# New operation figures in a list-scheduling planner, with the scaled x blocks and last-value copies on ScalarE

## The chip, the cores and the metric

The kernel runs on one core of one Trainium2 chip. A time is device microseconds (us) of one execution, the median of the runs shown. Engines: TensorE (PE in the profile; its weight loads are PEld), VectorE (DVE), ScalarE (ACT), GpSimd (POOL) and SyncE (SP), whose queue issues the transfers.

## The reference

One layer of a streaming encoder, for 1024 prompt positions and 32 sample positions over 512 cached ones, with shared weights. D_MODEL is 1024, eight heads of 64 in each of two mixers, a feed-forward width of 4096, all in fp32.

```
z = rmsnorm(x) @ w_in            # q,k,v of mixer A; indexer queries, key, head weights; q,k,v of mixer B; two gates
score = sum_h relu(q_i[h] @ k_i) * w_i[h];  idx = top_k(score)        # mixer A: which keys a query sees
o_a = softmax(q_a @ k_a[idx] / 8) @ v_a[idx]                          # with QK-norm and rotary
o_b = a @ v_b,  a = exp(log_sigmoid(s) - tail of softplus(s))         # mixer B: stick-breaking, s = q_b @ k_b / 8
h = x + W_out(sigmoid(g_A) * (o_a @ W_bA) + sigmoid(g_B) * (o_b @ W_bB))
y = h + W_down(relu(W_up rmsnorm(h))^2)
```

## The kernel before

All 1056 positions are one list of columns: eight tiles of 128 prompt positions and a ninth of 32 sample positions. Matmuls run on numbers split in two: a value is rounded to a shorter format (the high half, names ending in h) and the rest is kept as a second tile (the low half, names ending in l). A product is three matmuls, wh·xh, wh·xl and wl·xh. So each operand costs a rounding (ScalarE, or rarely VectorE or GpSimd) and a subtraction (VectorE or GpSimd) before TensorE can use it.

The stages: the index stage (first 70 us or so) normalises x block by block and projects it on the index queries and keys, in two parts; then mixer B's projections, index scores and a bitwise top-k search, mixer A's projections and gates; the attention of both mixers, in which gate products and the first part of the feed-forward network are woven in as filler; the rest of the feed-forward in a scheme with fewer products (quarter sums of the weights), to the end.

**What sets the order.** The kernel doesn't issue instructions as it is written. Every operation is recorded in a Plan (lines 109 to 425), which keeps data dependences between recorded operations and issues them by a list scheduler: `run` takes the engine that is free first, and from its ready operations the one with the best rank (FAST, PREP, MAIN, FILL, SLOW) and, within a rank, the first recorded. `cost` (line 223) gives each operation two numbers, how long it keeps its engine and how long until its result is there, by engine, operation and n, the elements in a partition; `after` adds SLACK, 300 ns, to each hand-over between engines. [...] The figures therefore decide nothing on the chip but the order on each engine; all operations are issued at line 416, which is why the profile has that line almost everywhere, and one goes by tiles.

**What the change touches.** `normalise` (line 717) loads eight blocks k of x for a group of tiles, in five groups of 128, 256, 128, 256 and 288 columns. Of each it makes xh, x scaled by g_mix and rounded, and xl = x*g_mix - xh on VectorE. For the first group and for k below 6 xh is made on ScalarE, for k = 6 and 7 of the other four groups on GpSimd, as a TENSOR_SCALAR. `index_weights` (805) loads the eight blocks of the index weights, rounds each (ih) and subtracts (il): il on GpSimd for odd k, on VectorE for even k. `index_projection` (821) multiplies them into bank s, after which VectorE makes the products ta and tb with the rotary tables, GpSimd adds them (rr, ka), TensorE transposes rr (bank t), and ScalarE and VectorE make both halves of qi. `unit` makes both halves of a 512-column weight block (wst to wh on ScalarE, wl on GpSimd). `spread_rs` (775) brings the reciprocal norms into rows: rsb is transposed into t, ScalarE copies it to rb, and VectorE multiplies the projections in bank pj by rb (zb). `project_v` (1030) copies the last column of each tile of v (vl, 128x8) from vt on VectorE.

## Time and profile before

| | |
|---|---|
| median of the runs shown | 1709.43 us (1708.81 to 1710.45) |
| the profiled execution | 1708.92 us, span 1707.1 us |
| mean granted TensorE clock | 1.000 |
| busy: PE, DVE, ACT, POOL | 1693.5, 1199.8, 1054.7, 887.8 us |
| transfers | 302.41 MB, mean 177 GB/s |

A row of instructions reads: line, engine, operation, out<-in by the program's names, shapes, count | busy us, mean ns of one | idle time of the engine just before, and what ended it. A row of the timeline begins with its start and its duration in us, and has the idle time before it in brackets. In the table of windows an engine's busy us stand beside the length of the window. Matmuls overlap, the end of one with the start of the next, so TensorE's starts tell more than its idle time.

### The profile page before, as it was taken

The numbers are of one execution on the slowest core, as the hardware profiler recorded it, in microseconds if no ns is written. First come the engines' busy times: TensorE is split into PE (matmuls) and PEld (weight loads), VectorE is DVE, ScalarE is ACT, GpSimd is POOL, SyncE is SP. The second block draws the span as 40 slices with busy tenths as digits, with TensorE's granted clock in tenths as the row PEclk, the third lists the DMA queues.
The fourth block names the chain that finished last, engine by engine and source line by source line (L and its number), as shares of the span: only waits on it lengthen the run. The fifth ranks groups of instructions, "written<-read, shape, count | busy, mean of one in ns | idle before, by whom it ended". The sixth has DMA issues, their size and how long they took to land.

```text
span 1707.1 us, 33451 instructions
## 1 busy us (share of the span) xinstructions
PE 1693.5 (99%) x11442; PEld 1574.0 (92%) x11442; DVE 1199.8 (70%) x2606; ACT 1054.7 (62%) x2319; POOL 887.8 (52%) x791
## 2 busy tenths in 40 slices
PE   8999999999999999999999999999999999999999
PEld 7989999999999988998888888889899999999998
DVE  8467788999656655987485776686765784767577
ACT  6656799873255777665465565575745675747473
POOL 5442343435433465235654443567667894646563
PEclk9999999999999999999999999999999999999999
DMA  7453453354577677544667465586576665555665
GB/s 225 122 149 102 140 160 99 114 164 147 163 197 196 166 207 236 156 146 132 195 210 231 144 206 179 187 276 210 193 249 181 193 183 175 173 173 173 173 188 172
DMA packets 195962, 302.41 MB, mean 177 GB/s; under 512 B 36048, under 2 KB 67376, under 8 KB 195792
## 3 DMA queue, kind: packets, MB, share of 16 engines
q1 hardware_dynamic: 195504, 299.94, 58.1%
q8 instruction: 90, 1.47, 0.4%
q14 instruction: 80, 0.66, 0.1%
q10 hardware_dynamic: 288, 0.34, 0.1%
HBM read 212.39 MB, written 87.70 MB: 176 GB/s over the span
## 4 chain that ended last, share of the span: by engine, by line
PE 92%; DVE 3%; POOL 1%; issue 1%; DMA 1%; ACT 1%; ACTq 0%; POOLq 0%; SPq 0%; DVEq 0%
PE pj L416 66%; PE s L416 14%; PE t L416 5%; PE o L416 4%; PE pd L416 2%; DVE p L416 1%; DVE xl L416 1%; POOL wl L416 1%; DVE tt L416 0%; DMA k<-cka 0%; DMA x<-xT 0%; DVE pj L416 0%; DVE wl L416 0%; POOL xh L416 0%; DVE more L416 0%
## 5 line engine op out<-in xcount | busy, mean ns | idle before, releaser
L416 PE MATMUL pj<-xh,wh 128*128 128x272 f32 (+2 forms) x1795 | 599.6, 335 | 1.2 <-DVE zb L416 0.8
L416 PE MATMUL pj<-xl,wh 128*128 128x272 f32 (+2 forms) x1795 | 599.2, 335 | 0.5 <-DVE xl L416 0.5
L416 PE MATMUL pj<-xh,wl 128*128 128x272 f32 (+2 forms) x1795 | 598.7, 334 | 0.0
L416 POOL TENSOR_TENSOR wl<-wst,wh 128x512 fp32r<-128x512 f32 x233 | 316.2, 1362 | 315.7 <-ACT wh L416 264.0
L416 PEld LDWEIGHTS pj<-xh,wh 128*128 128x128 f32 x1795 | 337.3, 188 | 30.5 <-DVE y L416 1.2
L416 PEld LDWEIGHTS pj<-xl,wh 128*128 128x128 f32 x1795 | 337.8, 188 | 29.3 <-DVE xl L416 0.7
L416 PEld LDWEIGHTS pj<-xh,wl 128*128 128x128 f32 x1795 | 337.4, 188 | 28.9
L416 ACT CAST wh<-wst 128x512 fp32r<-128x512 f32 x253 | 155.8, 620 | 113.2 <-PE pj L416 71.5
L416 POOL TENSOR_TENSOR wl<-raw,wh 128x512 fp32r<-128x512 f32 x98 | 132.2, 1354 | 87.8 <-ACT wh L416 61.4
L416 ACT CAST wh<-raw 128x512 fp32r<-128x512 f32 x148 | 91.4, 623 | 84.4 <-PE pj L416 54.6
L416 DVE TENSOR_TENSOR tt<-t,tt 128x512 fp32r<-128x512 f32 (+2 forms) x168 | 101.3, 621 | 45.3 <-ACT tt L416 44.3
L416 ACT CAST tt<-t 128x512 fp32r<-128x512 f32 (+2 forms) x168 | 86.5, 537 | 65.7 <-PE t L416 38.8
L416 ACT ACTIVATE junk<-score,cand 128x384 bf16<-128x384 f32 (+1 forms) x124 | 116.0, 935 | 3.2 <-DVE cand L416 1.0
L416 DVE TENSOR_TENSOR_SCAN p<-p 128x896 f32<-128x896 f32 (+6 forms) x66 | 101.2, 1562 | 9.8 <-ACT p L416 9.6
L416 PE MATMUL pj<-gl,wh 128*128 128x272 f32 x352 | 101.2, 288 | 0.0
L416 PE MATMUL pj<-gh,wh 128*128 128x272 f32 x352 | 101.2, 288 | 0.0
L416 PE MATMUL pj<-gh,wl 128*128 128x272 f32 x352 | 101.0, 289 | 0.0
L416 PEld LDWEIGHTS o<-tt,v 128*128 128x128 f32 x640 | 90.8, 188 | 8.3 <-DVE o L416 0.9
L416 PE MATMUL o<-tt,v 128*128 128x256 f32 (+1 forms) x640 | 97.7, 277 | 0.4 <-DVE tt L416 0.3
L416 PE MATMUL s<-k,q 128*128 128x384 f32 (+5 forms) x384 | 92.8, 353 | 0.3 <-issue 0.2
L416 POOL TENSOR_TENSOR wl<-rb,wh 128x512 fp32r<-128x512 f32 x49 | 68.4, 1397 | 42.0 <-ACT wh L416 41.9
L416 PE MATMUL s<-wh,xh 128*128 128x256 f32 x320 | 90.1, 285 | 0.0
(415 smaller groups left out, 4021.2 us busy)
## 6 DMA issues: line engine op xcount, KB each, us to landing
q<-dq SPq DMA_DIRECT2D x64, 256.0 KB, 5.2
raw<-w_up SPq DMA_DIRECT2D x52, 256.0 KB, 3.1
raw<-w_down SPq DMA_DIRECT2D x52, 256.0 KB, 3.0
k<-dk SPq DMA_DIRECT2D x48, 256.0 KB, 4.3
v<-dv SPq DMA_DIRECT2D x48, 256.0 KB, 3.5
wst<-w_g SPq DMA_DIRECT2D x42, 256.0 KB, 3.5
wst<-w_up SPq DMA_DIRECT2D x37, 256.0 KB, 2.9
wst<-w_down SPq DMA_DIRECT2D x36, 256.0 KB, 3.6
```

The source lines that it names most:

```text
L416: fn(*args, **kw)
```

## The change

Three things. First, figures in `cost`: VectorE's tensor_scalar has a fixed part of 200 ns for 160, its tensor_tensor_reduce 150 for 230; ScalarE's fixed part is 160 for 195 where the input lies in PSUM, and it is counted as free 110 ns (95 from SBUF) ahead of its result for 90; GpSimd's two-input operations are 200 + 2.14 n for 330 + 1.9 n, its tensor_scalar 270 + 0.85 n for 300 + 0.9 n. Second, all xh of `normalise` are made on ScalarE, eight more than before. Third, the four odd il go from GpSimd to VectorE, and the four copies vl from VectorE to ScalarE.

```
-            d = 300 + 0.9 * n if op in ("tensor_scalar", "memset") else 330 + 1.9 * n
-            return d - 30, d
+            d = 270 + 0.85 * n if op == "tensor_scalar" else 70 + 0.95 * n if op == "memset" else 200 + 2.14 * n
+            if op == "tensor_scalar" and out.dtype == F32R:
+                d = 230 + 3.2 * n
+            return d - 35, d
...
-                if sl[0] == 0 or k < 6:
+                if True:
                     nc.scalar.activation(xh, x32[:, kk, :n], AF.Copy, scale=self.gm[:, k:k + 1])
                 else:
                     nc.gpsimd.tensor_scalar(xh, x32[:, kk, :n], self.gm[:, k:k + 1], None, op0=ALU.mult)
...
-            (nc.gpsimd if k % 2 else nc.vector).tensor_sub(l, st, h.bitcast(F32))
+            nc.vector.tensor_sub(l, st, h.bitcast(F32))
...
-            nc.vector.tensor_copy(self.vl[:, p], vt[:, 127:SEQ:128])
+            nc.scalar.copy(self.vl[:, p], vt[:, 127:SEQ:128])
```

The number of matmuls and of transfers stays the same; their order does not. Three places follow, with the program's names and their buffer numbers (il1 is the low half of index weight block 1, xl0 the low half of x for the first 512 columns, x32 a loaded block pair, s a bank of the index projection). Lines are L416 before and L419 now.

VectorE in the first tile of the index stage, before:

```order
L416 TENSOR_TENSOR il0_245<-ist_243,ih0_244 128x328
L416 SCALAR_TENSOR_TENSOR xl0_222<-x32_242,gm_68,xh0_221 128x128 x2
L416 SCALAR_TENSOR_TENSOR xl0_222<-x32_249,gm_68,xh0_221 128x128
L416 TENSOR_TENSOR il2_252<-ist_250,ih2_251 128x328
L416 SCALAR_TENSOR_TENSOR xl0_222<-x32_249,gm_68,xh0_221 128x128
L416 SCALAR_TENSOR_TENSOR xl0_222<-x32_256,gm_68,xh0_221 128x128
L416 TENSOR_TENSOR il4_259<-ist_257,ih4_258 128x328
L416 SCALAR_TENSOR_TENSOR xl0_222<-x32_256,gm_68,xh0_221 128x128
L416 SCALAR_TENSOR_TENSOR xl0_222<-x32_263,gm_68,xh0_221 128x128
L416 TENSOR_TENSOR il6_266<-ist_264,ih6_265 128x328
```

VectorE there now:

```order
L419 TENSOR_TENSOR il1_248<-ist_246,ih1_247 128x328
L419 SCALAR_TENSOR_TENSOR xl0_222<-x32_242,gm_68,xh0_221 128x128 x2
L419 SCALAR_TENSOR_TENSOR xl0_222<-x32_249,gm_68,xh0_221 128x128
L419 TENSOR_TENSOR il2_252<-ist_250,ih2_251 128x328
L419 SCALAR_TENSOR_TENSOR xl0_222<-x32_249,gm_68,xh0_221 128x128
L419 TENSOR_TENSOR il3_255<-ist_253,ih3_254 128x328
L419 SCALAR_TENSOR_TENSOR xl0_222<-x32_256,gm_68,xh0_221 128x128 x2
L419 TENSOR_TENSOR il4_259<-ist_257,ih4_258 128x328
L419 TENSOR_TENSOR il5_262<-ist_260,ih5_261 128x328
L419 SCALAR_TENSOR_TENSOR xl0_222<-x32_263,gm_68,xh0_221 128x128 x2
L419 TENSOR_TENSOR il6_266<-ist_264,ih6_265 128x328
L419 TENSOR_TENSOR il7_269<-ist_267,ih7_268 128x328
```

The four odd il stand between the xl, and the last of them, il7, is the last of the tile's VectorE work; on TensorE its matmul now follows that of ih7 directly, where three matmuls of the next two tiles stood between.

GpSimd from its first il on, before:

```order
L416 TENSOR_TENSOR il7_269<-ist_267,ih7_268 128x328
L416 TENSOR_SCALAR xh0_221<-x32_278,gm_68 128x256 x2
L416 TENSOR_TENSOR rr_273<-ta_271,tb_272 128x256
L416 TENSOR_TENSOR ka_241<-ta_271,tb_272 128x64
L416 TENSOR_SCALAR xh0_221<-x32_292,gm_68 128x128
L416 TENSOR_TENSOR wl_343<-wst_341,wh_342 128x512
L416 TENSOR_TENSOR rr_282<-ta_280,tb_281 128x256
L416 TENSOR_TENSOR ka_241<-ta_280,tb_281 128x64
```

GpSimd there now:

```order
L419 TENSOR_TENSOR rr_273<-ta_271,tb_272 128x256
L419 TENSOR_TENSOR ka_241<-ta_271,tb_272 128x64
L419 TENSOR_TENSOR wl_343<-wst_341,wh_342 128x512
L419 TENSOR_TENSOR rr_282<-ta_280,tb_281 128x256
L419 TENSOR_TENSOR ka_241<-ta_280,tb_281 128x64
```

Both il and xh are gone, and what stood behind them follows at once; the eight xh stand on ScalarE behind those of blocks 4 and 5 of their group.

ScalarE where the reciprocal norms are spread (rb), with the casts of the next weights (wh), before:

```order
L416 COPY rb_225<-t_1161 128x32
L416 CAST qi_235<-t_407 64x2x32 x2
L416 CAST wh_1200<-wst_1199 128x512
L416 CAST wh_1215<-wst_1214 128x512
L416 COPY rb_225<-t_1160 128x512
L416 CAST zz_1177<-zb_1176 128x272
```

ScalarE there now:

```order
L419 COPY rb_225<-t_1162 128x32
L419 CAST qi_235<-t_407 64x2x32 x2
L419 CAST wh_1201<-wst_1200 128x512
L419 COPY rb_225<-t_1161 128x512
L419 CAST wh_1216<-wst_1215 128x512
L419 CAST zz_1178<-zb_1177 128x272
```

The second large copy to rb has moved ahead of a weight cast.

## The prediction

> **What bounds the kernel now.** I read the page first, then a table of windows by stage, then TensorE's waits, and last the timelines at the places where those waits fall. The page's busy line, and the chain that ended last:

> ```profile
> PE 1693.5 (99%) x11442; PEld 1574.0 (92%) x11442; DVE 1199.8 (70%) x2606; ACT 1054.7 (62%) x2319; POOL 887.8 (52%) x791
> PE 92%; DVE 3%; POOL 1%; issue 1%; DMA 1%; ACT 1%; ACTq 0%; POOLq 0%; SPq 0%; DVEq 0%
> ```

> TensorE is the bound: 1693.5 of 1707.1 us, at a granted clock of 1.00. The change issues the same matmuls in another order, so it can move the time only by the 13.6 us in which TensorE is idle, and by the little that such a pause hides. Where those lie, by stage (length, then each engine's busy us; the last window runs 0.9 us past the end of the span):

> ```profile
> 0.00:8.50 8.50, 3.22 (x11) 2.92 (x12) 4.40 (x14) 5.25 (x14) 2.15 (x6) 1.00 0.77 220
> 8.50:40.00 31.50, 29.50 (x183) 26.70 (x182) 29.74 (x60) 21.93 (x59) 23.28 (x27) 1.00 0.74 229
> 40.00:100.00 60.00, 59.16 (x428) 55.50 (x428) 31.49 (x93) 35.48 (x89) 23.94 (x31) 1.00 0.49 138
> 100.00:520.00 420.00, 420.00 (x2884) 390.97 (x2884) 326.66 (x860) 271.06 (x658) 167.62 (x162) 1.00 0.48 142
> 520.00:800.00 280.00, 279.27 (x1853) 254.72 (x1853) 206.27 (x383) 187.32 (x417) 125.55 (x119) 1.00 0.64 181
> 800.00:1400.00 600.00, 599.99 (x3702) 542.14 (x3701) 399.02 (x769) 355.32 (x697) 374.71 (x305) 1.00 0.63 201
> 1400.00:1708.00 308.00, 302.34 (x2393) 301.08 (x2391) 202.24 (x432) 178.35 (x390) 170.58 (x144) 1.00 0.59 176
> ```

> The columns are PE, PEld, DVE, ACT, POOL. The first 8.5 us lose 5.28 us to the first loads, which the change does not touch. The index stage to 40 us idles 2.00 us, and VectorE is busy there for 29.74 of 31.50 us: it is what TensorE waits for. From 40 to 100 us 0.84 us are idle, from 100 to 520 nothing, from 520 to 800 0.73 us, from 800 to 1400 0.01, and the rest is the last output and one pause. The longest of TensorE's waits say the same (total us, times, longest):

> ```profile
> PE s L416 <- ACT xh L416: 5.6, 2, 5.3
> PE s L416 <- DVE xl L416: 1.3, 2, 0.7
> PE pj L416 <- DVE zb L416: 0.8, 1, 0.8
> PE pj L416 <- DVE xl L416: 0.5, 1, 0.5
> PE o L416 <- DVE tt L416: 0.3, 1, 0.3
> ```

> The two waits for xl, the low half of x, are worth more than their idle time. On TensorE's timeline, at three places of the index stage:

> ```profile
> 16.57 0.31 PE L416 MATMUL s<-il,xh 128*128 128x328 f32 x1
> 17.00 0.42 PE L416 MATMUL s<-ih,xl 128*128 128x328 f32 x1
> ...
> 24.11 0.31 PE L416 MATMUL s<-ih,xl 128*128 128x328 f32 x1
> 25.06 0.42 PE L416 MATMUL s<-ih,xl 128*128 128x328 f32 x1 [0.64 <-DVE xl L416]
> 25.31 0.31 PE L416 MATMUL s<-ih,xh 128*128 128x328 f32 x1
> ...
> 31.40 0.31 PE L416 MATMUL s<-il,xh 128*128 128x328 f32 x1
> 32.36 0.57 PE L416 MATMUL s<-ih,xl 128*128 128x328 f32 x2 [0.65 <-DVE xl L416]
> ```

> The reader should look at starts, not at idle time. A matmul follows the one before by 0.15 us when nothing waits (25.31, then 25.46). From 24.11 to 25.06 are 0.95 us, so 0.80 are lost where 0.64 show as idle, and the next start comes 0.10 late as well: 0.90 in all, 0.26 more than is shown. By the same count 32.36 loses 0.91 and 17.00, which shows no idle time, 0.28 + 0.10 = 0.38.

> **Part by part. The x blocks.** Why is xl late? GpSimd and VectorE at those places:

> ```profile
> 21.47 0.69 POOL L416 TENSOR_SCALAR xh<-x,gm 128x128 fp32r<-128x128 f32 x1
> 22.13 2.59 POOL L416 TENSOR_TENSOR wl<-wst,wh 128x512 fp32r<-128x512 f32 x2
> ...
> 17.07 0.34 DVE L416 SCALAR_TENSOR_TENSOR xl<-x,gm,xh 128x128 fp32r<-128x128 f32 x1
> ...
> 22.20 1.38 DVE L416 SCALAR_TENSOR_TENSOR xl<-x,gm,xh 128x128 fp32r<-128x128 f32 x1
> ...
> 30.63 1.39 POOL L416 TENSOR_TENSOR wl<-wst,wh 128x512 fp32r<-128x512 f32 x1
> ...
> 30.41 1.89 DVE L416 SCALAR_TENSOR_TENSOR xl<-x,gm,xh 128x256 fp32r<-128x256 f32 x2
> ```

> The xl of block 7 needs GpSimd's xh, which ends at 22.16; by then GpSimd is in wl, and xl takes 1.38 us where the same form takes 0.34 undisturbed. That is 1.04 us, and the next xl, for which TensorE waits at 25.06, comes that much later. At 30.63 the two xl of blocks 6 and 7 meet another wl, which had queued behind two xh, and end at 32.30: that is the wait at 32.36. With the eight xh on ScalarE both causes go: xh is ready earlier, and GpSimd does its wl ahead of these xl. I take both waits and the 0.38 at 17.00 (an xl behind GpSimd's xh too) as gone: -0.90 - 0.91 - 0.38 = -2.19. VectorE stays nearly full here, so other rr, ka and wl can still hold some xl: the bounds are 0 and -2.19, and I keep -2.0 because the 1.04 us given back at 22.20 are more than either wait.

> What it costs on ScalarE: eight instructions, at most 0.532 us each by the row below, 4.3 us. ScalarE is busy for 21.93 of the stage's 31.50 us, so 9.6 us are free and I put it at nothing. Without that cover (ScalarE's own queue: qi, wi and the wh of w_ib stand behind them) up to 4.3 us would be late; w_ib is first used after 44 us.

> ```profile
> L416 ACT ACTIVATE xh<-x,gm 128x288 fp32r<-128x288 f32 x6 | 3.0, 532 | 1.3 <-DMA x<-xT 1.3
> L416 POOL TENSOR_TENSOR il<-ist,ih 128x328 fp32r<-128x328 f32 x4 | 3.8, 946 | 6.7 <-ACT ih L416 6.7
> L416 DVE TENSOR_TENSOR il<-ist,ih 128x328 fp32r<-128x328 f32 x4 | 2.0, 490 | 0.0
> ...
> 10.03 0.89 POOL L416 TENSOR_TENSOR il<-ist,ih 128x328 fp32r<-128x328 f32 x1 [0.47 <-ACT ih L416]
> ...
> 10.04 1.03 DVE L416 SCALAR_TENSOR_TENSOR xl<-x,gm,xh 128x128 fp32r<-128x128 f32 x1
> ```

> **The il.** Four low halves of the index weights leave GpSimd (3.8 us) and add 4 x 0.490 = 1.96 us to VectorE, in the first tile, where nothing covers VectorE. Against that, an xl beside GpSimd's il took 1.03 instead of 0.34: 0.69 back, and four il stand in that tile, so at most 4 x 0.69 = 2.8. VectorE comes out between -0.8 and +1.96. But the last il is now behind all of VectorE's work of the tile, and the row order has TensorE use it directly after ih7, where three matmuls of the next tiles stood between: I take +0.3, with ends -0.8 and +1.96.

> [...]

> ```profile
> 13.79 0.47 DVE L416 SCALAR_TENSOR_TENSOR xl<-x,gm,xh 128x256 fp32r<-128x256 f32 x1
> ...
> 13.85 2.11 POOL L416 TENSOR_SCALAR xh<-x,gm 128x256 fp32r<-128x256 f32 x2 [2.93 <-DMA x<-xT]
> ```

> This xl has two SBUF inputs, ran beside xh and took 0.47 all the same. So I count no hold-up beside xh as given back; if xl were held there, all of the stage's waits would go, which is the first rival.

> **The copies of the last values.** Four VectorE copies leave:

> ```profile
> L416 DVE COPY vl<-vt x4: 172/801/951, 120.7 to 253.1; 128x8 f32<-128x8 f32 x4
> ```

> At most 3.8 us of VectorE, all between 120 and 254 us, where TensorE is never idle (420.00 of 420.00). Zero, cover or no cover; on ScalarE they come between casts for TensorE, and a wait of 0.3 us each (the o wait above) would be the upper end, 1.2.

> **The new figures.** They reorder without adding work, most of all in the attention from some 470 to 965 us. One place where TensorE waits and the order changes in a clear way is the end of the first q projection:

> ```profile
> 84.06 0.60 PE L416 MATMUL t<-ident,rsb 128*128 128x128 f32 x4
> 86.06 0.50 PE L416 MATMUL pj<-xh,wh 128*128 128x512 f32 x1 [0.83 <-DVE zb L416]
> ...
> 84.31 0.62 ACT L416 CAST wh<-wst 128x512 fp32r<-128x512 f32 x1 [0.93 <-PE pj L416]
> 84.95 0.58 ACT L416 COPY rb<-t 128x512 f32<-128x512 f32 x1
> ```

> The transposes end at 84.66; rb starts at 84.95 because a cast of a weight is ahead of it. In the new order rb comes first: -0.3 (ends 0 and -0.93, the wait with its late second start). What is late next is zb, after rb. For the attention I take zero: its waits in 520 to 800 us are 0.73 idle, a new order removes some and makes others, so -1.3 to +1.3 (0.73 and two hidden 0.26).

> Sum: -2.0 + 0.3 + 0 - 0.3 + 0 = -2.0; the profiled execution took 1708.92 us (span 1707.1, 1.8 around it), which makes 1706.9. The median of the runs shown is 0.51 above that execution, so I predict 1707.4, 0.12% below 1709.43. About 0.2%, 3.4 us, is what a measurement of this kernel can tell from no change, so my forecast is: within it, on the fast side.

> **Rivals.** *All of the stage's waits go* (faster by over 0.2%): VectorE is freed by more than I count, every xl beside an xh included, and the 2.00 idle plus 0.26 for each of four shown waits (3.0) go, with 0.93 at 86 us: 1709.43 - 3.9 = 1705.5. [...] For it: VectorE is busy for 94% of that stage. Against it: rr, ka and wl stay on GpSimd and go on holding xl.

> *Nothing is gained*: the first tile costs the full 1.96 and the xl are held elsewhere by the same wl, which only move: 1709.43 - 2.0 + 1.96, some 1709.4. For it: GpSimd's wl are as many as before. Against it: the 1.03 beside il.

> *The attention runs out of margin* (slower): GpSimd's TENSOR_TENSOR is now counted by 200 + 2.14 n, 902 ns for 128x328, while that row's mean is 946. A low half that comes late is met by TensorE in order, and each such wait costs 0.3 (the o wait above) + 0.26 = 0.56. It decides only where the lateness passes the 300 ns of slack that the plan adds to each hand-over. To come out 0.2% slower it takes (3.4 + 2.0) / 0.56, ten such waits; with eleven it is 1707.4 + 6.2 = 1713.6. For it: TensorE's order changes most there. Against it: before, TensorE idled 0.73 us in 280 with the same slack.

> **How the numbers follow.** My forecast 0.42, all waits gone 0.30, nothing gained 0.18, attention 0.10. Faster by over 0.2% takes the first rival and a little of mine: 0.32; slower is the attention alone, nearly: 0.09; the rest, 0.59, is within. The range reaches from the first rival less 1.3 for the attention, 1704.2, and 0.6 below that for the il's better end, 1703.6, to nothing gained plus 1.3, 1710.7; it leaves out the attention's case and the far end of the first rival.

> **What would show it.** Right: in the changed profile PE's idle time in 8.5 to 40 us near 0.8 instead of 2.00, no wait for xl over 0.3 us after 20 us, VectorE's xl mean near 0.4 for 128x128, the wait for zb at 86 us shorter by 0.3, nothing idle from 100 to 520 us, and 0.7 +- 0.5 from 520 to 800. Wrong: a wait for il or xl of over 1 us in the first 13 us (the il), ScalarE's xh as TensorE's releaser after 15 us (the cover), or several idle us from 520 to 965 (the attention).

## The result, and the profile after

The changed kernel takes 1718.92 us (median of 6 runs, 1716.23 to 1723.23) against 1709.67 us for the kernel before (6 runs, 1708.81 to 1710.45). The ratio is 1.0059, 95% interval 1.0049 to 1.0069: slower by 9 us, where I had said 1707.4 and a range up to 1710.7. The profiled execution took 1717.92 us, its span 1716.1.

The busy line of the page after, then the table of windows of the changed kernel by the same stages (PE, PEld, DVE, ACT, POOL, the granted clock, the DMA share, GB/s; the last window is 9 us longer):

```profile
PE 1696.2 (99%) x11442; PEld 1577.4 (92%) x11442; DVE 1195.0 (70%) x2606; ACT 1057.8 (62%) x2331; POOL 883.7 (51%) x779
```

```profile
8.50:40.00 31.50, 29.13 (x177) 26.43 (x177) 28.46 (x59) 23.73 (x65) 14.07 (x17) 1.00 0.73 229
40.00:100.00 60.00, 59.67 (x432) 55.96 (x431) 31.55 (x94) 36.24 (x91) 22.58 (x30) 1.00 0.47 136
100.00:520.00 420.00, 417.17 (x2854) 387.54 (x2852) 330.01 (x856) 269.91 (x660) 165.18 (x162) 1.00 0.49 142
520.00:800.00 280.00, 277.12 (x1851) 254.88 (x1850) 198.38 (x379) 184.18 (x412) 132.31 (x117) 0.99 0.63 176
800.00:1400.00 600.00, 599.61 (x3672) 540.34 (x3671) 393.64 (x762) 353.76 (x690) 370.52 (x303) 1.00 0.63 201
1400.00:1717.00 317.00, 310.29 (x2457) 309.04 (x2455) 208.36 (x443) 184.71 (x405) 178.84 (x150) 1.00 0.59 175
```

TensorE's idle time went from 2.00 to 2.37 us in the index stage, from 0.84 to 0.33 up to 100 us, from 0 to 2.83 up to 520 us, from 0.73 to 2.88 up to 800 us and from 0.01 to 0.39 up to 1400 us. The clock column shows something new: 0.99 in one stage. TensorE's waits in the changed kernel:

```profile
PE s L419 <- ACT xh L419: 6.3, 2, 5.3
PE pj L419 <- POOL wl L419: 1.9, 2, 1.5
PE o L419 <- POOL vcs L419: 1.8, 1, 1.8
PE t L419 <- DVE az L419: 1.4, 1, 1.4
PE s L419 <- DVE xl L419: 1.1, 3, 0.7
PE t L419 <- POOL qk L419: 0.7, 1, 0.7
PE o L419 <- DVE o L419: 0.7, 1, 0.7
```

Few and single pauses, then, at places where the kernel before has none. Counting lost starts as in the prediction (the time from one matmul's start to the next, over the normal step), the matmul of the same number starts 0.7 us later than before at 45 us, 0.2 at 97, 3.5 at 446, 8.0 at 1394, and the last one 9.0 us later. Five losses of 0.8 us or more after 100 us (at 371, 397, 550, 712 and 1411 us) make 7.0 of it, and a stretch at half clock behind the one at 550 makes 1.55 more (last section). The longest losses are 1.61 us at 371 us, 2.02 at 550 and 1.69 at 1411; each has its own story, and the three timelines of the changed kernel show them. At 371, 550 and 1411 us, on TensorE and the engines beside it:

```profile
367.29 1.78 DVE L419 TENSOR_SCALAR pen<-score,tfa 128x1024 f32<-128x1024 f32 x1
368.48 0.58 ACT L419 CAST az<-t 128x512 fp32r<-128x512 f32 x1
369.10 1.66 DVE L419 CUSTOM_DVE_ANT_0 pen<-pen,score 128x1024 f32<-128x1024 f32 x1
369.63 2.25 POOL L419 TENSOR_TENSOR wl<-wst,wh 128x512 fp32r<-128x512 f32 x1
370.69 0.68 DVE L419 TENSOR_TENSOR az<-t,az 128x512 fp32r<-128x512 f32 x1
371.43 0.66 PE L419 MATMUL t<-ident,vt 128*128 128x128 f32 x4 [1.45 <-DVE az L419]
...
546.38 3.80 DVE L419 TENSOR_TENSOR_SCAN p<-p 128x384 f32<-128x384 f32 x5
546.98 4.41 POOL L419 TENSOR_TENSOR vcs<-vc,vcs 128x256 fp32r<-128x256 f32 x2 [4.20 <-ACT vcs L419]
550.75 0.63 PE L419 MATMUL o<-tt,vcs 128*128 128x64 f32 x4 [1.77 <-POOL vcs L419]
...
1408.43 1.23 POOL L419 TENSOR_TENSOR xl<-ut,xh 128x272 fp32r<-128x272 f32 x1
1408.95 1.26 DVE L419 TENSOR_TENSOR wl<-raw,wh 128x512 fp32r<-128x512 f32 x1
1409.62 1.72 POOL L419 TENSOR_TENSOR wl<-wst,wh 128x512 fp32r<-128x512 f32 x1
1411.39 0.39 PE L419 MATMUL pj<-xh,wl 128*128 128x272 f32 x1 [1.53 <-POOL wl L419]
```

At 371 us TensorE's transposes need the bank that az reads, and az stands in VectorE's queue behind the top-k's last pair of operations. That pair is itself slow here: 1.78 and 1.66 us with GpSimd busy beside it all the time, where the same two take 0.74 and 1.21 in the kernel before (at 371.04 and 372.85 us; GpSimd's qk, started at 372.89 beside the second, took 1.78 there, where 0.75 is usual). The difference, 1.49 us, is nearly the whole loss, so GpSimd's work beside the pair may be as much the cause as the place of az in the queue; no run separates the two. At 550 us GpSimd's low half of the cached v takes 3.72 us, the first of the two, beside a run of five VectorE scans (the other fifteen take 0.73 to 0.90). At 1411 us GpSimd and VectorE make low halves side by side: GpSimd's wl takes 1.72 us where 1.3 is usual, and the xl ahead of it in its queue 1.23 where 0.77 is. Together that is 0.9 of the loss of 1.69; the rest is that GpSimd comes to this wl late.

In the index stage the waits moved, and one new one came, by a way the prediction had put at nothing:

```profile
24.14 2.81 POOL L419 TENSOR_TENSOR wl<-wst,wh 128x512 fp32r<-128x512 f32 x2 [0.30 <-ACT wh L419]
25.29 1.95 DVE L419 SCALAR_TENSOR_TENSOR xl<-x,gm,xh 128x256 fp32r<-128x256 f32 x2
27.26 0.42 DVE L419 TENSOR_TENSOR qi<-t,qi 64x256 fp32r<-64x256 f32 x1
27.71 0.37 ACT L419 CAST qi<-t 64x256 fp32r<-64x256 f32 x1 [2.75 <-DVE qi L419]
28.18 2.60 ACT L419 ACTIVATE xh<-x,gm 128x256 fp32r<-128x256 f32 x6
29.37 0.49 DVE L419 TENSOR_TENSOR tb<-s,is 128x320 f32<-128x320 f32 x1
30.00 0.39 PE L419 MATMUL s<-ih,xh 128*128 128x328 f32 x1 [0.95 <-ACT xh L419]
```

GpSimd's wl now meet the two xl at 25.29 (1.95 us for both, where an xl of this form takes 0.48 undisturbed); VectorE's qi comes late; ScalarE sits idle for 2.75 us in front of its own qi, which starts at 27.71; and the six xh of two column groups start behind it, at 28.18. The profile ends TensorE's wait at 30.00 with one of these xh, the fourth, done at 29.93. But TensorE also waited there for VectorE's tb, which reads a bank s and ended at 29.86, so the xh alone cost less than 0.1 us of it.

### The profile page after: what moved, and what is told of

Read it like the earlier page. It is cut to its first block, busy times and chain, and to the rows that moved or that the text cites. A ratio compares the mean times of both kernels' runs of the same rounds, so it can differ in the third digit from the quotient of the medians.

```text
span 1716.1 us, 33438 instructions
## 1 busy us (share of the span) xinstructions
PE 1696.2 (99%) x11442; PEld 1577.4 (92%) x11442; DVE 1195.0 (70%) x2606; ACT 1057.8 (62%) x2331; POOL 883.7 (51%) x779
## 5 line engine op out<-in xcount | busy, mean ns | idle before, releaser
L419 PE MATMUL pj<-xh,wl 128*128 128x272 f32 (+2 forms) x1795 | 599.5, 335 | 1.5 <-POOL wl L419 1.5
L419 PE MATMUL pj<-xh,wh 128*128 128x272 f32 (+2 forms) x1795 | 599.6, 335 | 0.7 <-DVE zb L419 0.3
L419 PE MATMUL pj<-xl,wh 128*128 128x272 f32 (+2 forms) x1795 | 599.0, 334 | 0.0
L419 POOL TENSOR_TENSOR wl<-wst,wh 128x512 fp32r<-128x512 f32 x233 | 323.0, 1391 | 337.2 <-ACT wh L419 277.7
L419 PEld LDWEIGHTS pj<-xh,wl 128*128 128x128 f32 x1795 | 338.2, 189 | 30.4 <-POOL wl L419 1.8
L419 PEld LDWEIGHTS pj<-xh,wh 128*128 128x128 f32 x1795 | 337.9, 189 | 30.4 <-DVE y L419 1.0
L419 PEld LDWEIGHTS pj<-xl,wh 128*128 128x128 f32 x1795 | 338.5, 189 | 28.2
L419 ACT CAST wh<-wst 128x512 fp32r<-128x512 f32 x253 | 155.8, 620 | 128.1 <-PE pj L419 75.7
L419 POOL TENSOR_TENSOR wl<-raw,wh 128x512 fp32r<-128x512 f32 x98 | 134.1, 1374 | 95.9 <-ACT wh L419 72.7
L419 ACT CAST wh<-raw 128x512 fp32r<-128x512 f32 x148 | 91.2, 623 | 80.5 <-PE pj L419 49.1
L419 ACT CAST tt<-t 128x512 fp32r<-128x512 f32 (+2 forms) x168 | 85.8, 539 | 81.1 <-PE t L419 53.1
L419 DVE TENSOR_TENSOR tt<-t,tt 128x512 fp32r<-128x512 f32 (+2 forms) x168 | 100.5, 622 | 44.2 <-ACT tt L419 42.9
L419 ACT ACTIVATE junk<-score,cand 128x384 bf16<-128x384 f32 (+1 forms) x124 | 115.9, 935 | 6.5 <-DVE cand L419 4.3
L419 DVE TENSOR_TENSOR_SCAN p<-p 128x896 f32<-128x896 f32 (+6 forms) x66 | 98.5, 1519 | 10.9 <-ACT p L419 10.8
L419 PE MATMUL pj<-gl,wh 128*128 128x272 f32 x352 | 101.4, 288 | 0.0
L419 PE MATMUL pj<-gh,wh 128*128 128x272 f32 x352 | 101.2, 288 | 0.0
L419 PE MATMUL pj<-gh,wl 128*128 128x272 f32 x352 | 100.8, 289 | 0.0
L419 PE MATMUL o<-tt,v 128*128 128x256 f32 (+1 forms) x640 | 98.4, 279 | 0.7 <-DVE o L419 0.7
L419 PEld LDWEIGHTS o<-tt,v 128*128 128x128 f32 x640 | 91.1, 188 | 7.1 <-DVE o L419 0.9
L419 PE MATMUL s<-k,q 128*128 128x384 f32 (+5 forms) x384 | 93.4, 354 | 0.4 <-DMA k<-dk 0.4
L419 PE MATMUL s<-wh,xh 128*128 128x256 f32 x320 | 90.3, 285 | 0.1
L419 PE MATMUL s<-wh,xl 128*128 128x256 f32 x320 | 90.3, 283 | 0.0
```

What stands on the lines that cost most here:

```text
L419: fn(*args, **kw)
```

## The experiments

Three theories. **A**: the new figures mislead the plan, which puts late low halves where TensorE meets them. **B**: the moves cost the time, the x blocks on ScalarE above all. **C**: every change of the plan's numbers or instructions draws another order, with waits at places of its own, and the loss is that of this draw. All times are medians beside runs of the kernel before on the same chip; its own medians were 1709.3 to 1709.9.

**Which part of the change?** One half of the change each, and two orders drawn from the kernel before by a number that says nothing false of an engine. `figures_only` is the kernel before with the new cost function, `moves_only` the changed kernel with the old one.

```diff
# nudge_act, cost() of the kernel before
-            d = 195 + 0.84 * n + (190 if "accum_out" in kw else 0)
+            d = 200 + 0.84 * n + (190 if "accum_out" in kw else 0)
# nudge_slack (310), nudge_slack_290, slack_320: the kernel before
-SLACK, STORE = 300, 1000
+SLACK, STORE = 310, 1000
```

> The kernel before with all new figures and none of the three moves. Theory A (the new figures mislead the plan: attention and projections are put in an order whose low halves come late): 1715 to 1722 us, with some 4 to 7 us of TensorE idle between 100 and 965 us and no wait for ScalarE's xh near 30 us. Theory B (the moves do it, the x blocks on ScalarE above all): 1709 to 1711 us, with the same waits between 100 and 800 us as before. Theory C (the order of before is a lucky draw, and any change of the plan's numbers or instructions draws another, with waits at places of its own): 1711 to 1720 us, with waits that do not lie at the places of the changed kernel.

> The changed kernel with the figures of before: only the three moves. Theory A: 1708 to 1711 us. Theory B: 1715 to 1722 us, with the wait for ScalarE's xh near 30 us. Theory C: 1711 to 1720 us, waits at places of its own outside the index stage.

> The kernel before, with one figure of the plan moved by 5 ns: ScalarE's fixed part 200 instead of 195. No instruction goes to another engine. Theories A and B: 1709.7 within 1.5 us, since 5 ns say nothing false of an engine. Theory C: the same loss as in the changed kernel is possible, 1711 to 1720 us, with two or more TensorE waits of over 0.5 us between 40 and 965 us that the kernel before does not have.

> The kernel before, with the plan's slack of each hand-over 310 ns instead of 300. No instruction goes to another engine. Theories A and B: 1709.7 within 1.5 us, since more slack can only make the plan safer. Theory C: 1711 to 1720 us, with waits at places of its own.

Measured: figures alone 1719.72 us (ratio 1.0066, 1.0049 to 1.0083), moves alone 1717.19 (1.0046, 1.0031 to 1.0061), ScalarE 5 ns slower in the plan 1710.16 (1.0005, 0.9996 to 1.0015), 10 ns more slack 1716.53 (1.0047, 1.0031 to 1.0062). Each half alone costs what both cost together, and so does a number that has nothing to do with either. A and B as the whole cause fall; B's sign, a wait for ScalarE's xh near 30 us, is missing in `moves_only`. C stands, but not in all that it expected: the waits of `figures_only` do not lie at places of their own. From 302 us on its matmuls stand in the same order as those of the changed kernel and its five longest waits are at the same matmuls, so it is that draw once more. With the 5 ns (`nudge_act`) the time is the one that A and B expected. TensorE's waits with a slack of 310 ns read like those of the changed kernel:

```profile
PE o L416 <- POOL vcs L416: 2.1, 2, 1.6
PE t L416 <- DVE vs L416: 1.6, 1, 1.6
PE s L416 <- DMA q<-dq: 1.0, 1, 1.0
PE t L416 <- POOL qk L416: 0.9, 2, 0.7
```

**The moves without a new order.** The order of the kernel before is kept; only the engine is changed at the moment of issue, after the plan has placed the instruction as before. For the x blocks (il and vl likewise):

```diff
                     nc.gpsimd.tensor_scalar(xh, x32[:, kk, :n], self.gm[:, k:k + 1], None, op0=ALU.mult)
+                    nc.put(nc.nc.scalar.activation, xh, x32[:, kk, :n], AF.Copy, scale=self.gm[:, k:k + 1])
# put(): the node just recorded is issued with this call instead
+    def put(self, fn, *args, **kw):
+        self.nodes[-1].call = (fn, list(args), kw)
```

> The order of the kernel before is kept as it is; only the sixteen instructions of the three moves are issued on their new engine, each where it stood among all others. Theory C (the new order costs the time, not the moves): 1707.5 to 1710.5 us, no TensorE wait after 100 us that the kernel before does not have; by the forecast's own terms (x blocks -2.0, il +0.3) 1708.0. Theory B (the moves cost it): 1713 us or more, with TensorE idle over 3 us in 8.5 to 40 us, waiting for ScalarE's xh or for xl.

> As the run with all moves in place, but the eight scaled x blocks alone on ScalarE. If their own price is what was forecast: 1707.7 us, and the waits for xl at 17, 25 and 32 us shorter by 0.3 or more each. If ScalarE is no free place (xh behind casts that wait for VectorE): the wait for xl goes, but ScalarE's xh or a later xl is waited for instead, and the time is 1709 to 1711 us.

Measured: all moves 1709.01 us (ratio 0.9998, 0.9989 to 1.0008), the x blocks alone 1708.35 (0.9992, 0.9983 to 1.0002). B falls for good: by this interval the moves by themselves cost at most 1.4 us. It would also allow the 1.7 us of gain that the terms for x blocks and il add up to; the trace shows less, a lead of 0.83 us over the kernel before at 45 us, 0.26 of which stood at 8 us already. Two windows with all moves in place, the index stage and the stage in which the vl copies now come from ScalarE:

```profile
8.50:40.00 31.50, 29.48 (x187) 28.01 (x187) 28.26 (x62) 25.47 (x69) 14.12 (x17) 1.00 0.75 237
...
100.00:520.00 420.00, 420.00 (x2885) 391.03 (x2885) 325.31 (x857) 271.56 (x662) 167.89 (x162) 1.00 0.48 142
```

The index stage idles 2.02 us instead of 2.00. The waits at 17 and 32 us are gone, but the one at 25 us has grown and two of 0.4 follow at 33.5 and 34.5. The run with the x blocks alone shows the one at 25 us:

```profile
21.52 1.19 ACT L416 ACTIVATE xh<-x,gm 128x256 fp32r<-128x256 f32 x3
22.61 0.60 ACT L416 CAST wh<-wst 128x512 fp32r<-128x512 f32 x1
23.12 0.74 ACT L416 CAST qi<-t 64x256 fp32r<-64x256 f32 x2
23.90 0.86 DVE L416 TENSOR_TENSOR qi<-t,qi 64x256 fp32r<-64x256 f32 x2 [0.96 <-ACT qi L416]
24.79 1.22 DVE L416 SCALAR_TENSOR_TENSOR xl<-x,gm,xh 128x256 fp32r<-128x256 f32 x2
25.60 0.19 PEld L416 LDWEIGHTS s<-ih,xl 128*128 128x128 f32 x1 [1.49 <-DVE xl L416]
```

The two xl now take 1.22 us together (beside GpSimd's rr and ka; 0.48 each is undisturbed). They stand on VectorE behind qi, whose cast stands on ScalarE behind wh and three xh, where two stood before. The first of these xh starts at 21.52 us instead of 20.81, behind a wi that waited for VectorE, and qi's cast at 23.12 instead of 22.51: 1.39 us are lost at the xl where 0.80 were.

**One wait taken out of the changed kernel.** Its order is kept; two low halves of the cached v go to VectorE.

```diff
             self.split(vcs[:, :, 0:HD], vcs[:, :, HD:], vc[:, j % 2])
+            if u == 1 and not is_a and j < 2:
+                nc.put(nc.nc.vector.tensor_sub, vcs[:, :, HD:], vc[:, j % 2], vcs[:, :, 0:HD].bitcast(F32))
```

> The order of the changed kernel is kept; two low halves of the cached v (128x256) near 547 us are issued on VectorE instead of GpSimd, between the scans that stood beside them. If VectorE's scans hold GpSimd there: the wait of 2.0 us at 550 us goes, and the half-clock window of 3.4 us behind it with it, 1.7 us more; 1714.5 to 1716.5 us. If those low halves are late for another reason, or the scans they now delay by 0.9 us are waited for instead: 1718 to 1720 us.

Measured: 1715.31 us (ratio 1.0039, 1.0024 to 1.0054), 3.6 below the changed kernel by medians of 4 and 6 runs whose ranges overlap. Matmul by matmul the two profiled executions are surer: the changed kernel falls behind by 2.03 us at the pause and by 1.55 in the 3.4 us after it. Each low half takes 0.39 us between the scans, and TensorE no longer waits at 549 us:

```profile
547.37 0.39 DVE L419 TENSOR_TENSOR vcs<-vc,vcs 128x256 fp32r<-128x256 f32 x1
...
548.95 0.53 PE L419 MATMUL o<-tt,vcs 128*128 128x64 f32 x4
```

So the low halves were late because GpSimd took 3.72 us for the first of them beside the scans, and the pause was worth more than its 2.0 us; the rest is the clock, below.

**The wait at 371 us.** On top of the edit above, the top-k's pair over 128x1024 is first issued behind az, ta, tb and ss (`az_first`), then left out (`no_pen`: the kernel leaves out this refinement of one tile's threshold and copies the unrefined one).

```diff
# az_first, in issue(): n.id in self.late for the pair of t == 7
-        fn(*args, **kw)
+        if n.id in self.late:
+            self.kept.append(n.call)
+        else:
+            fn(*args, **kw)
+        if self.kept and args and n.eng == DVE and args[0].tensor.name.startswith("ss"):
+            for f, x, y in self.kept:
+                f(*x, **y)
+            self.kept = []
# no_pen, in top_k() for t == 7, behind the first and the second of the pair
+                        nc.put(lambda: None)
+                        nc.put(nc.nc.vector.tensor_copy, low[:m, j:j + 1], tf[:m, j:j + 1])
```

> The changed kernel's order with the two cached-v low halves on VectorE as before, and on VectorE the top-k's last pair of operations over 128x1024 issued behind az, ta, tb and ss instead of ahead of them near 367 us. If az is late only because it stands behind that pair: the 1.6 us lost at 371 us go, 1713.7 us. If VectorE is simply full in that stretch: the wait goes over to the low half vs or to tb within 6 us, with 1 us or more, and the time is 1715.3 us as without the edit.

> The changed kernel's order with the two cached-v low halves on VectorE, and VectorE's pair of top-k operations over 128x1024 near 367 us (1.78 and 1.66 us) left out, a copy of one column in its place; the threshold of that one tile is then the unrefined one. If VectorE is full in that stretch and every other order of the same work only moves the wait: the 1.6 us at 371 us go, no other wait of over 0.5 us stands within 8 us, 1713.6 us. If the wait is made by something else on the chain of az (ScalarE's cast, the transposes): 1715.3 us as with the pair.

Measured: 1716.04 us with the pair behind az (1.0040, 1.0025 to 1.0055), no gain over 1715.31; 1713.87 without the pair (1.0028, 1.0017 to 1.0039), 1.4 less, which the spread of the runs does not tell from nothing; by the starts in the profiled executions 1.66 us are saved at 371 us. With the pair moved, the loss moves too, to 375 us:

```profile
368.90 0.69 DVE L423 TENSOR_TENSOR az<-t,az 128x512 fp32r<-128x512 f32 x1 [0.83 <-ACT az L423]
370.50 1.14 DVE L426 TENSOR_SCALAR pen<-score,tfa 128x1024 f32<-128x1024 f32 x1
371.67 1.23 DVE L426 CUSTOM_DVE_ANT_0 pen<-pen,score 128x1024 f32<-128x1024 f32 x1
374.21 0.42 DVE L423 TENSOR_TENSOR vs<-t,vs 128x256 fp32r<-128x256 f32 x1
374.78 0.77 PE L423 MATMUL t<-ident,vt 128*128 128x128 f32 x5 [1.75 <-DVE az L423]
```

Without the pair no matmul between 330 and 400 us waits for over 0.28 us. VectorE has little room in that stretch, 1.2 to 1.9 us of 25.2 in three orders. The same 25.2 us in the changed kernel, in the kernel before, and in the order drawn with a slack of 290 ns (below):

```profile
348.00:373.20 25.20, 23.65 (x165) 21.58 (x164) 23.28 (x78) 19.64 (x47) 8.27 (x7) 1.00 0.54 154
```

```profile
348.00:373.20 25.20, 25.20 (x179) 23.38 (x179) 23.79 (x83) 21.72 (x50) 8.72 (x9) 1.00 0.60 176
```

```profile
348.00:373.20 25.20, 25.20 (x188) 23.95 (x189) 24.01 (x85) 21.53 (x50) 7.95 (x8) 1.00 0.57 161
```

VectorE (the third engine) is busy for 92 to 95% in all three, counting what its operations take longer beside GpSimd's (3.44 us for the pair against 1.95). In two of them everything comes in time with little to spare; in the changed kernel az does not, and leaving out the 3.4 us of the pair got rid of the wait where this one move of it did not. Whether the pair in its place, but at the 1.95 us that it takes in the kernel before, would do is untested.

**More draws.** Are the new figures a worse set as such? The changed kernel with other slacks (`new_slack_290`, `new_slack_310`), with one engine's figures put back (`pool_old` for GpSimd, `act_old`, `dve_old`), both (`pool_old_290`), and the kernel before with other slacks. The edits are the SLACK line above and the lines of cost() in the diff, undone.

> The kernel before with the plan's slack of each hand-over 290 ns instead of 300. Theory A (false figures mislead the plan): 1709.7 within 1.5 us, since 10 ns less slack is little beside the 300. Theory C (every other order is a new draw): anywhere from 1709 to 1720 us, with waits at places of its own.

> The kernel before with a slack of 320 ns. Theory C (each order a draw, whatever the figures): 1705 to 1722 us. If the old figures are good as such and only 310 was unlucky: 1709.7 within 1.5 us. No wait for GpSimd's wl of over 1 us near 1410 us, since none of the five orders with the old figures has one.

> The changed kernel (moves and figures) with the slack of each hand-over 290 ns instead of 300: another order, drawn with the new figures. Theory A (the new figures mislead the plan): 1716 to 1722 us again, with waits at 371, 550 or 1411 us again. Theory C (the loss is that of one draw): anywhere from 1705 to 1722 us; under 1712 us speaks for C, since the figures are the same.

> The same with a slack of 310 ns. Theory A: 1716 to 1722 us. Theory C: anywhere from 1705 to 1722 us. If this and the run with 290 both come out over 1715 us, C loses ground: then four draws of four with the new figures are bad, against two of four with the old.

> The changed kernel with GpSimd's figures as before; ScalarE's and VectorE's new. Four orders of four with the new figures wait for GpSimd's wl near 1410 us (1.3 to 1.7 us lost), none of five with the old figures does. If GpSimd's figures make that wait, it is gone here and the waits of 800 us to the end are as before (0.7 us and small ones); the time up to 800 us is a draw of its own: 1706 to 1718 us. If they do not, 1.3 to 1.7 us are lost near 1410 us again.

> The changed kernel with ScalarE's figures as before. If ScalarE's figures (35 ns less for every operation that reads PSUM) make the wait for wl near 1410 us, it is gone here: 1706 to 1718 us by the draw up to 800 us. If not, 1.3 to 1.7 us are lost there again, 1708 to 1720 us.

> The changed kernel with VectorE's two figures as before. The two operations concerned stand in the top-k and the index stage, none near 1410 us: the wait for wl near 1410 us should stay (1.3 to 1.7 us lost), and the time is 1708 to 1720 us by the draw up to 800 us. If VectorE's figures made the loss at 371 us, nothing over 0.5 us is lost within 10 us of it.

> The changed kernel with GpSimd's figures as before and a slack of 290 ns: one more draw, from the best set so far of those that hold the moves. Theory C: anywhere from 1705 to 1722 us. If GpSimd's old figures are what makes a good order: 1706 to 1710 us again.

All fourteen orders, with the start losses over 0.25 us of two places in the profiled execution (matmuls 2430 to 2470, some 371 to 378 us, and 9060 to 9100, some 1405 to 1412 us):

| order | moves | figures | slack | us | ratio, 95% | lost near 371 | lost near 1410 |
|---|---|---|---|---|---|---|---|
| nudge_slack_290 | old | old | 290 | 1706.61 | 0.9977 to 0.9995 | 0 | 0 |
| kernel before | old | old | 300 | 1709.67 | | 0 | 0.7 (xl) |
| nudge_act | old | old, ACT +5 | 300 | 1710.16 | 0.9996 to 1.0015 | 0.5 | 0 |
| nudge_slack | old | old | 310 | 1716.53 | 1.0031 to 1.0062 | 3.0 | 0 |
| slack_320 | old | old | 320 | 1725.63 | 1.0077 to 1.0107 | 5.7 | 0.3 (wl) |
| moves_only | new | old | 300 | 1717.19 | 1.0031 to 1.0061 | 4.7 | 0.7 (xl) |
| pool_old_290 | new | new, GpSimd old | 290 | 1706.43 | 0.9973 to 0.9992 | 0 | 0 |
| pool_old | new | new, GpSimd old | 300 | 1708.55 | 0.9981 to 1.0000 | 0 | 0 |
| act_old | new | new, ScalarE old | 300 | 1714.02 | 1.0016 to 1.0037 | 1.9 | 0.8 (pd) |
| dve_old | new | new, VectorE old | 300 | 1713.47 | 1.0016 to 1.0035 | 1.9 | 1.7 (wl) |
| new_slack_290 | new | new | 290 | 1710.70 | 1.0000 to 1.0019 | 0 | 1.3 (wl) |
| changed kernel | new | new | 300 | 1718.92 | 1.0049 to 1.0069 | 1.9 | 1.7 (wl) |
| figures_only | old | new | 300 | 1719.72 | 1.0049 to 1.0083 | 1.9 | 1.7 (wl) |
| new_slack_310 | new | new | 310 | 1719.36 | 1.0041 to 1.0074 | 2.3 | 1.7 (wl) |

C holds in the main: the old figures alone span 1706.6 to 1725.6 us. Its ranges were too narrow on both sides (1706.61 with 290 ns, where 1709 to 1720 was expected, and 1725.63 with 320 ns, where 1705 to 1722 was). But not all is chance, and the fourteen are not fourteen independent draws, as `figures_only` shows. The wait for GpSimd's wl near 1410 us stands in all five orders that have both ScalarE's and GpSimd's new figures, and in none of the nine others with more than 0.3 us (slack_320): 1.3 to 1.7 us are lost where 0 to 0.8 is usual, so some 1 us of the 9 belongs to the figures as such. Putting GpSimd's figures back made the order faster both times (by 10.4 and 4.3 us). And in all three sets of figures less slack never came out measurably slower, and mostly faster, against what more slack is for. Whether that is a rule of the plan or still chance, fourteen orders do not settle, and why 10 ns turn the order at 371 us stays open.

**A version that beats both.** The order drawn with a slack of 290 ns, kept, and the moves put in place as above.

> The order drawn from the kernel before with a slack of 290 ns (1706.6 us), kept as it is, with the sixteen instructions of the three moves on their new engines in place. The index stage of that order loses 2.2 us to an xl at 26.7 us and 0.6 at 33.1. If the moves free VectorE and GpSimd there as forecast: 1 to 2 us less, 1705.0 us. If the waits only go to other xl, as in the order of before: 1706 to 1707 us.

Measured: 1706.33 us, ratio 0.9982 (0.9972 to 0.9992): 3 us under the kernel before, but no more than that order gains without the moves (1706.61), and the same as pool_old_290 (1706.43, 0.9983).

## Why the prediction was wrong, step by step

**The step that failed most** is "For the attention I take zero: its waits in 520 to 800 us are 0.73 idle, a new order removes some and makes others, so -1.3 to +1.3." It is a term of the right kind, mis-sized: from 97 us to its end the changed kernel falls 8.8 us behind the kernel before. The kernel before is a good draw: it had almost no waits after 100 us, so a new order could remove next to nothing and only make some. The other orders lost up to 5.7 us near 371 us alone, and my bound was taken from the waits of that one good order. I had also looked in the wrong place: 100 to 520 us, where I put "nothing idle" because TensorE was busy 420.00 of 420.00, is where VectorE, behind the index stage, had least to spare (92 to 95% busy from 348 to 373 us), and 3.3 of the 9 us were lost there by 446 us. The clock was no term at all: the prediction prices a pause by its idle time and a little more, and the one at 550 us cost 1.55 us besides, at half clock.

**The slower rival** had the direction and the wrong mechanism. It wanted ten or more waits of 0.56 us from low halves that come late by more than the slack. What came were five pauses of 0.8 to 2.0 us after 100 us, from what stood ahead in the queues of VectorE (az behind the pair at 371 us) and GpSimd (wl behind xl at 1411), and from a low half that took 3.72 us on GpSimd beside scans; and more slack made it worse (1716.53 and 1725.63 with 310 and 320 ns), not better. Its chance of 0.10 was far too small.

**The x blocks**: -2.0 forecast, no gain in the trace of one execution (the interval of the times would still allow it): alone and in place, TensorE's matmuls start 0.17 us earlier at 45 us than in the kernel before, and 0.28 of lead stood already at 8 us. The failed step is "ScalarE is busy for 21.93 of the stage's 31.50 us, so 9.6 us are free and I put it at nothing". I named the queue behind the xh (qi, wi, wh) and then priced it by the engine's free time. Not the free time counted but what stood ahead in the queue: three xh and a wh, with a late wi ahead of them, put off qi's cast by 0.6 us, qi put off xl, and 1.39 us were lost at that xl. In the new order ScalarE's xh is what the profile names at 30 us, the sign of a failed cover that the prediction gave, but VectorE's tb ended only 0.07 us before it. A reading was wrong too. The xl of 0.47 us beside GpSimd's xh, from which the prediction took it that xh does not hold xl, had started before that xh (13.79 against 13.85); two xl of the kernel before that started inside an xh (15.09 and 29.79 us) took 0.70 us, where 0.48 is undisturbed; two that started 0.16 and 0.25 us before an xh's end (29.39 and 30.41) took 0.48 and 0.47.

**The il**: +0.3 forecast. At 14 us the run with the x blocks alone stands 0.34 us behind the kernel before, the run with the il too 0.24 ahead: -0.58 by one execution each, nearer the end of -0.8 than the value taken. **The vl copies**: zero, right (420.00 of 420.00 with all moves in place). **rb ahead of the cast**: -0.3 forecast, the loss at 86 us went from 1.00 to 0.49, so -0.5; right in kind, and within its ends.

## What to carry to other kernels

Where a planner orders the work by a table of costs, a change of the table is a new draw of the whole order, and a change of one operation's engine is one too: time several draws (a slack of 10 ns more or less is enough) before crediting or blaming the numbers, and test a move with the order held fast. An order that shows almost no waits is near the best of its kind (here the best two of the others were 3 us faster), so its own small waits do not bound what another order loses: look for the stretch where a helper engine is busy for over 90%, idle TensorE or not. Price work added to an engine by what stands behind it in that engine's queue and who waits for that, not by the engine's idle share.

## What the runs showed of the hardware that was not expected

**A pause of 1.8 us was followed by a window of 3.4 us at half clock.** The windows around the pause at 550 us in the changed kernel, and in figures_only, which has the same pause in the same order of matmuls:

```profile
548.92:552.34 3.42, 1.65 (x15) 1.59 (x15) 1.40 (x3) 0.81 (x3) 2.47 (x2) 1.00 0.99 237
552.34:555.75 3.41, 3.41 (x19) 3.41 (x18) 1.40 (x2) 0.98 (x3) 1.49 (x2) 0.50 0.42 96
```

```profile
549.48:552.90 3.42, 2.45 (x21) 2.45 (x22) 1.40 (x2) 0.77 (x2) 1.60 (x2) 1.00 1.09 205
552.90:556.31 3.41, 3.41 (x22) 3.05 (x22) 1.71 (x4) 1.61 (x4) 3.10 (x3) 1.00 0.65 180
```

**GpSimd's two-input operations took longer beside VectorE's scans.** The 128x256 low half took 3.72 us beside five scans, and 0.73 to 0.90 at the other fifteen places in the changed kernel. Over all twenty traces GpSimd's two-input operations over 128x512 took 1.26 to 1.33 us where VectorE did nothing beside them (964 of them); where scans ran for over half of their time (396) they took 2.20 at the median, from 1.27 to 4.69. The prediction knew only the other direction, an xl that took 1.38 us for 0.34 beside GpSimd's wl.
